# Residual stream and the outputs of w_out, w_down and the last projection with tokens on partitions, in a three-block fp32 kernel on one core

## The chip, the cores and the metric

One core of a Trainium2 chip runs the whole program in one launch. The metric is the device time in microseconds (us); a time is the median of several runs of the same kernel. The profile is of one execution. Engines are named as the profile does: PE (TensorE, matmul), PEld (its weight load), DVE (VectorE), ACT (ScalarE), POOL (GpSimd), SP (SyncE, which issues most DMAs).

## The reference, cut to what matters

256 tokens of width D = 2048 pass two layers of the first block and one of the second. All is float32.

```python
for l in range(2):                              # first block
    u = rms_norm(h, norm_pre_mix[l])
    p = u @ w_in[l]                             # four groups of mixers read p
    mixed = concat(o_ret, o_hgrn, o_ml, o_rw) @ w_out[l]             # 2048 x 2048
    h = h + rms_norm(mixed, norm_post_mix[l])
    u = rms_norm(h, norm_pre_ffn[l])
    ffn = (silu(u @ w_gate[l]) * (u @ w_up[l])) @ w_down[l]           # w_down: 5632 x 2048
    h = h + rms_norm(ffn, norm_post_ffn[l])
shift, scale, gate = split(c @ w_ada + b_ada)   # second block
u = rms_norm(h, g_pre) * (1 + scale) + shift
proj = u @ w_in_2                               # two attentions read it and give `merged`
return h + gate * rms_norm(merged @ w_out_2, g_post)
# rms_norm(x, g) = x * rsqrt(mean(x * x) + 1e-6) * g
```

## The kernel before, in words

**Weights.** Each weight is read once from HBM in chunks of 128 x 1024 (512 KB). `prep` sends a chunk by SP's queue to `raw` (a ring of 3), ScalarE rounds it to fp32r as `hi` (L104), VectorE subtracts for `lo` (L105); `hi` and `lo` are rings of 4. An activation is split the same way, so that a product is wh·xh + wh·xl + wl·xh.

**Two forms of a product.** In `stream_a` a block of 128 x 128 weights is stationary and the activations move, high and low part side by side: one matmul of 512 columns (L151) and one of 256 (L152) per block, output features on partitions, tokens in the free dimension. A job with `one` True makes three matmuls of 256 columns in their place (L147 to L149). In `stream_b` the activations are stationary and 512 columns of weights move, three matmuls for each half of the tokens (L195 to L197): tokens on partitions, two banks of 512 columns at the end. Before the change it serves the value and gate projections of the mixers.

**The residual stream.** `h` is [128 features, 16 blocks k, 256 tokens]. w_out, w_down and the last projection run as 16 jobs of 128 output features. `collect` takes each job's bank: ScalarE squares it (L219), GpSimd and VectorE add the squares up, VectorE writes the bank times the gain into `mo` (tiles named `uq`). At the end the matmul `mean` with a constant 1/D sums over partitions (L233); `rstd` makes the root as a tile R of 128 x 256 by Ln and Exp on ScalarE and one Newton step on VectorE (L252 to L263), while `busy` gives TensorE 20 matmuls on constants. Then `entry` feeds the next stage k by k: `residual` multiplies `mo` with R on GpSimd (on VectorE for k = 0, L313) and adds to `h` on VectorE (L314), `u_tile` makes the two parts of u, on ScalarE (L299) and VectorE (L300). The root of the *new* norm isn't waited for: u goes unscaled into the matmuls, and the results are scaled when their banks are drained; `late` squares `h` (L219) after the first stage's last group.

**The first stage of a consumer** (four jobs side by side, so that 4 k are 16 pairs of matmuls, a *group*) is the place where TensorE follows `feed`: `FIRST` has four groups of four k. Layer 0 has no residual: x comes by SP's queue in the layout of `h`, and `START` has five groups, the first with one k. The second block's entry uses tiles `u1` of its own with a column more for the shift.

**What sets the order.** The program is written stage by stage and ordered by a scheduler ahead of time; `issue_after` pins single instructions behind others.

Of the kernel before, what the change touches and what calls it, by code (L numbers as in the profile page):

```python
# [17 lines left out]
D = 2048  # L18
# [10 lines left out]
class Squares:  # L29


    def __init__(self):
        self.parts, self.bank, self.begun = [], None, False


class Core:
# [53 lines left out]
    def prep(self, srcs, n, pool=False):  # L90
# [14 lines left out]
        self.last = (nc.gpsimd if pool else nc.vector).tensor_tensor(lo[:, :n], raw[:, :n], hi[:, :n].bitcast(F32), op=OP.subtract)  # L105
        return hi, lo

    def stream_a(self, jobs, rhs, phases, feed=None, late=None, load=None, whole=None, bank=None):
# [10 lines left out]
        for ph in phases:  # L119
# [7 lines left out]
            with ExitStack() as cx:  # L127
# [3 lines left out]
                for i in range(0, len(jobs), step):  # L131
                    if soon and i and made:
                        cx.enter_context(self.tc.issue_after(self.squared.ins))
                    hi, lo = self.prep(w[i:i + step], n, soon and i > 0 and len(made) > 0)
                    parts += [(hi[:, j * n:(j + 1) * n], lo[:, j * n:(j + 1) * n]) for j in range(min(step, len(jobs) - i))]
# [47 lines left out]
    def stream_b(self, w, nk, lhs, done):  # L183

        nc = self.nc
        banks = [self.sbank() for _ in range(2)]
        for k0 in range(0, nk, 2):
            hi, lo = self.prep([w[:, k0 * 512:(k0 + 2) * 512]], 1024)
            for j in range(2):
                k = k0 + j  # L190
                x = lhs(k)
                for tt in range(2):
                    xh, xl = x[:, tt * 128:(tt + 1) * 128], x[:, 256 + tt * 128:384 + tt * 128]
                    wh, wl = hi[:, j * 512:(j + 1) * 512], lo[:, j * 512:(j + 1) * 512]
                    nc.tensor.matmul(banks[tt], xh, wh, start=(k == 0), stop=False)  # L195
                    nc.tensor.matmul(banks[tt], xh, wl, start=False, stop=False)  # L196
                    nc.tensor.matmul(banks[tt], xl, wh, start=False, stop=(k == nk - 1))  # L197
        for tt in range(2):
            done(tt, banks[tt])
# [15 lines left out]
    def square(self, acc, x, i, n):  # L215

        nc = self.nc
        sq = self.t(self.ev, [128, 256], f"acc{i}", 1) if i < 2 else self.t(self.ev, [128, 256], "sq", 2)
        self.squared = nc.scalar.square(sq, x)  # L219
        if i < 2 or i == n - 1:  # L220
            acc.parts.append(sq)
        else:
# [1874 lines left out]
```

## Time and profile before

| what | before |
|---|---|
| median of 3 runs | 3568.17 us (3563.52 to 3569.63) |
| profiled execution, time | 3567.99 us |
| profiled execution, span | 3565.9 us |
| mean granted TensorE clock | 0.989 of full speed |
| PE busy | 3481.8 us, 98% |
| DVE, ACT, POOL busy | 70%, 50%, 19% |
| weights read from HBM | 645.78 MB, 182 GB/s over the span |

The span runs from the first to the last instruction; the time has a little around it. A share of busy time is an average over stages: TensorE stands still at few places only, and each of them is short, so the table tells little of them and the timeline has to.

### The profile page before, as it was taken

How to read it: one execution, taken by the hardware profiler on the slowest of the kernel's cores; microseconds unless marked ns; L12 is line 12 of the kernel's file. 1: busy time of each engine (PE TensorE's matmuls, PEld its weight loads, DVE VectorE, ACT ScalarE, POOL GpSimd, SP SyncE). 2: the span in 40 equal slices, each digit the busy share in tenths (PEclk: the TensorE clock that was granted, in tenths of full speed). 3: DMA queues.
4: the chain of work that ended last, by engine and by line, in shares of the span. 5: the costliest groups of instructions: out<-in, count | busy, mean ns of one | idle time of the engine just before them, and what ended most of it. 6: DMA issues, size and time to landing. Idle time of an engine off the chain costs nothing.

```text
span 3565.9 us, 61722 instructions
## 1 busy us (share of the span) xinstructions
PE 3481.8 (98%) x23680; PEld 3055.1 (86%) x23680; DVE 2483.3 (70%) x4456; ACT 1769.4 (50%) x2957; POOL 660.2 (19%) x824
## 2 busy tenths in 40 slices
PE   8999999999999999999999899999999999999997
PEld 8788987888888888878888788888888899988886
DVE  7777877777776557887786877776556766765555
ACT  5553545544444444655455544444444654555443
POOL 2123303211110004122320411111003212100001
PEclk9999999999999999999999999999999999999999
DMA  6335555677776664424455577777664655445554
GB/s 207 114 107 165 181 169 152 222 235 235 237 236 211 206 195 153 157 81 148 158 169 183 168 234 234 238 235 227 205 201 150 197 166 167 140 136 186 187 184 141
DMA packets 209368, 652.46 MB, mean 183 GB/s; under 512 B 24176, under 2 KB 27152, under 8 KB 209072
## 3 DMA queue, kind: packets, MB, share of 16 engines
q1 hardware_dynamic: 169664, 577.84, 50.7%
q10 hardware_dynamic: 39408, 70.67, 6.2%
q8 instruction: 186, 3.05, 0.3%
q14 instruction: 110, 0.90, 0.1%
HBM read 645.78 MB, written 2.65 MB: 182 GB/s over the span
## 4 chain that ended last, share of the span: by engine, by line
PE 85%; DVE 8%; DMA 2%; ACT 2%; issue 2%; POOL 0%; ACTq 0%; SPq 0%; DVEq 0%; POOLq 0%
PE s L151 34%; PE s L152 17%; PE s L147 5%; PE s L149 5%; PE s L148 5%; PE s L195 4%; PE s L196 3%; PE s L197 3%; DVE lo L105 2%; DVE h L314 1%; ACT hi L104 1%; DMA raw<-in_wina_dram 1%; PE g L148 1%; PE g L149 1%; DVE uq L300 1%
## 5 line engine op out<-in xcount | busy, mean ns | idle before, releaser
L105 DVE TENSOR_TENSOR lo<-raw,hi 128x1024 fp32r<-128x1024 f32 (+1 forms) x1101 | 1383.9, 1258 | 834.4 <-ACT hi L104 827.4
L104 ACT CAST hi<-raw 128x1024 fp32r<-128x1024 f32 (+1 forms) x1105 | 1141.6, 1035 | 1275.5 <-PE s L151 676.1
L151 PE MATMUL s<-uq,hi 128*128 128x512 f32 x3344 | 1177.6, 394 | 3.9 <-ACT hid L211 3.9
L152 PE MATMUL s<-uq,lo 128*128 128x256 f32 x3344 | 934.6, 279 | 0.0
L151 PEld LDWEIGHTS s<-uq,hi 128*128 128x128 f32 x3344 | 628.3, 188 | 154.4 <-ACT hid L211 4.5
L152 PEld LDWEIGHTS s<-uq,lo 128*128 128x128 f32 x3344 | 628.4, 188 | 0.2
L151 PE MATMUL s<-hid,hi 128*128 128x512 f32 x1320 | 466.5, 396 | 0.0
L147 PE MATMUL s<-uq,hi 128*128 128x256 f32 x1456 | 418.6, 288 | 1.3 <-ACT hi L104 0.5
L148 PE MATMUL s<-uq,hi 128*128 128x256 f32 x1456 | 417.7, 287 | 0.0
L149 PE MATMUL s<-uq,lo 128*128 128x256 f32 x1456 | 417.4, 287 | 0.0
L152 PE MATMUL s<-hid,lo 128*128 128x256 f32 x1320 | 372.2, 282 | 0.0
L151 PEld LDWEIGHTS s<-hid,hi 128*128 128x128 f32 x1320 | 248.0, 188 | 60.1
L147 PEld LDWEIGHTS s<-uq,hi 128*128 128x128 f32 x1456 | 275.2, 189 | 9.3 <-issue 6.6
L149 PEld LDWEIGHTS s<-uq,lo 128*128 128x128 f32 x1456 | 275.3, 189 | 6.1 <-issue 5.1
L148 PEld LDWEIGHTS s<-uq,hi 128*128 128x128 f32 x1456 | 275.4, 189 | 5.9 <-issue 4.8
L152 PEld LDWEIGHTS s<-hid,lo 128*128 128x128 f32 x1320 | 247.9, 188 | 0.0
L196 PE MATMUL s<-lo,uq 128*128 128x512 f32 x608 | 245.4, 404 | 1.0 <-DVE lo L105 1.0
L195 PE MATMUL s<-hi,uq 128*128 128x512 f32 x608 | 242.8, 406 | 0.6 <-ACT vo L1867 0.4
L197 PE MATMUL s<-hi,uq 128*128 128x512 f32 x608 | 243.1, 401 | 0.0
L223 POOL TENSOR_TENSOR acc<-acc,sq 128x256 f32<-128x256 f32 x70 | 84.4, 1206 | 791.3 <-ACT sq L219 791.3
L373 POOL TENSOR_TENSOR gs<-e,R 128x256 f32<-128x256 f32 x88 | 81.0, 921 | 443.8 <-DVE e L206 408.3
L379 POOL TENSOR_TENSOR e<-e,R 128x256 f32<-128x256 f32 x88 | 76.1, 864 | 367.5 <-DVE e L206 367.5
(638 smaller groups left out, 5230.1 us busy)
## 6 DMA issues: line engine op xcount, KB each, us to landing
raw<-in_wg_dram SPq DMA_DIRECT2D x168, 512.0 KB, 4.5
raw<-in_wu_dram SPq DMA_DIRECT2D x168, 512.0 KB, 4.7
raw<-in_wd_dram SPq DMA_DIRECT2D x160, 512.0 KB, 3.6
raw<-in_wina_dram SPq DMA_DIRECT2D x154, 512.0 KB, 3.9
raw<-in_win2a_dram SPq DMA_DIRECT2D x130, 512.0 KB, 4.2
raw<-in_winb_dram SPq DMA_DIRECT2D x96, 512.0 KB, 3.6
raw<-in_wout_dram SPq DMA_DIRECT2D x96, 512.0 KB, 4.5
aw<-in_wada_dram ACTq DMA_DIRECT2D x192, 256.0 KB, 5.0
```

The source lines that it names most:

```text
L104: self.last_hi = nc.scalar.copy(hi[:, :n], raw[:, :n])
L105: self.last = (nc.gpsimd if pool else nc.vector).tensor_tensor(lo[:, :n], raw[:, :n], hi[:, :n].bitcast(F32), op=OP.subtract)
L147: nc.tensor.matmul(banks[i][:, 0:n], wh, x[:, 0:n], start=first, stop=False)
L148: nc.tensor.matmul(banks[i][:, 0:n], wh, x[:, n:2 * n], start=False, stop=False)
L149: nc.tensor.matmul(banks[i][:, 0:n], wl, x[:, 0:n], start=False, stop=last)
L151: nc.tensor.matmul(banks[i], wh, x, start=first, stop=False)
L152: nc.tensor.matmul(banks[i][:, 0:256], wl, x[:, 0:256], start=False, stop=last)
L195: nc.tensor.matmul(banks[tt], xh, wh, start=(k == 0), stop=False)
L196: nc.tensor.matmul(banks[tt], xh, wl, start=False, stop=False)
L197: nc.tensor.matmul(banks[tt], xl, wh, start=False, stop=(k == nk - 1))
L223: (nc.vector if i % 2 else nc.gpsimd).tensor_tensor(acc.parts[i % 2], acc.parts[i % 2], sq, op=OP.add)
L373: nc.gpsimd.tensor_tensor(g, e, rget(), op=OP.mult)
```

## The change

`h` becomes [128 tokens, 2 halves, 2048], and so does `mo`. w_out, w_down and the last projection become four blocks of 512 output features through `stream_b` (`rows_b`), with the weights laid out for it. ScalarE squares a bank and sums the squares along its row in the same instruction (`accum_out`); the root is a column [128,1] for each half of the tokens. The gain comes by a DMA as a tile of 128 x 512 for each block. The residual is one VectorE instruction (`h = mo * r + h`). For u the tokens must be back in the free dimension: `entry` transposes `h` on TensorE, 32 times 128 x 128 per entry, and u is read from the banks; `h` is squared in eight instructions of 128 x 512. The root of the entry is a column too and is spread to the tile R by one matmul (`Rstd`). In layer 0 x still comes transposed, into slots of `raw`, and `h` comes once more as one DMA of 2.1 MB on ScalarE's queue. `busy` drops from 20 to 10 matmuls. The second block keeps the scaled transposes as `hs`, and its output gain goes to DRAM once to be read back as a row.

```diff
+    def stream_b(self, w, ks, lhs, done, banks=None, apart=False, beside=None):
...
+            order = [(j, tt) for j in range(2) for tt in range(2)]
+            for j, tt in sorted(order, key=lambda x: x[1]) if apart and end else order:
...
+    def rows_b(self, ws, nk, lhs, gains, acc, sides, orders=None, beside=None):
+        nc = self.nc
+        self.new_mo()
+        for i in range(4):
+            gain = self.t(self.ev, [128, 512], "gain", 1)
+            with self.tc.issue_after(self.last_hi.ins):
+                nc.scalar.dma_start(gain, gains(i).partition_broadcast(128))
...
+            def done(tt, bank, i=i, gain=gain):
+                sq = self.t(self.ev, [128, 512], "sq", 1)
+                nc.scalar.activation(sq, bank, AF.Square, accum_out=acc.ss[:, tt, i:i + 1])
+                def keep():
+                    nc.vector.tensor_tensor(self.mo[tt][:, i * 512:(i + 1) * 512], bank, gain, op=OP.mult)
+                if i < 3:
+                    keep()
+                else:
+                    acc.later.append(keep)
...
+                if i == 3:
+                    x, t, y = acc.x[:, tt, 1:2], acc.x[:, tt, 2:3], acc.r[:, tt:tt + 1]
+                    nc.vector.scalar_tensor_tensor(x, acc.ss[:, tt, 3:4], 1.0 / D, acc.x[:, tt, 0:1], op0=OP.mult, op1=OP.add)
+                    nc.scalar.activation(y, x, AF.Ln)
+                    self.rooted = nc.scalar.activation(y, y, AF.Exp, scale=-0.5)
+                    self.newton(y, x, t)
+            side = sides[i]
+            self.stream_b(ws[i], orders[i] if orders else range(nk), lhs, done, None if side is None else [self.g(side), self.g(side)], i == 3, beside)
...
+    def warm(self):
+        with self.tc.issue_after(self.last_mm.ins):
+            self.busy(10)
...
+    def residual(self, acc, c):
+        for tt in range(2):
+            self.nc.vector.scalar_tensor_tensor(self.h[:, tt, c], self.mo[tt][:, c], acc.r[:, tt:tt + 1], self.h[:, tt, c], op0=OP.mult, op1=OP.add)
...
         def feed(ph):
-            for k in ph:
-                if r is not None:
-                    self.residual(k, r, k == 0)
-                made = self.u_tile(u(k) if u else self.uk(k), self.h[:, k], w[:, k:k + 1], r is not None and k == 0)
-            return made if r is not None else ()
+            if x is None and ph[0] == 8:
+                for f in mo.later:
+                    f()
+            for i, k in enumerate(ph):
+                if x is None:
+                    if i == 0 or k == 1:
+                        self.residual(mo, slice(k * 128, 128 if k == 0 else (ph[-1] + 1) * 128))
+                    if i % 2 == 0:
+                        g = self.g()
+                    turned[k] = v = g[:, i % 2 * 256:i % 2 * 256 + 256]
+                    for tt in range(2):
+                        nc.tensor.transpose(v[:, tt * 128:(tt + 1) * 128], self.h[:, tt, k * 128:(k + 1) * 128], self.ident)
...
         def late():
-            for k in range(KT):
-                self.square(acc, self.h[:, k], k, KT)
+            for tt in range(2):
+                for i in range(4):
+                    sq = self.t(self.ev, [128, 512], "sq", 1)
+                    nc.scalar.activation(sq, self.h[:, tt, i * 512:(i + 1) * 512], AF.Square, accum_out=acc.ss[:, tt, i:i + 1])
             rs()
...
+        if ph[0] == 8:
+            with tc.issue_after(K.last_hi.ins):
+                nc.scalar.dma_start(K.h, A["xn"])
```

How the scheduler has ordered the work around the first seam (w_out of layer 0 into its feed-forward) is seen in the instruction lists. VectorE before, from the end of the root (R) on; `uq<-h` are halves of u:

```order
L263 SCALAR_TENSOR_TENSOR R<-tmp,R 128x256
L313 TENSOR_TENSOR tmp<-uq,R 128x256
L314 TENSOR_TENSOR h<-h,tmp 128x256 x2
L297 TENSOR_SCALAR uq<-h,nrm 128x256
L300 SCALAR_TENSOR_TENSOR uq<-h,nrm,uq 128x256
L314 TENSOR_TENSOR h<-h,tmp 128x256
L300 SCALAR_TENSOR_TENSOR uq<-h,nrm,uq 128x256
```

VectorE after, at the same place (`sr` is the new root, `uq<-g` a low half of u read from transposes, `nx` and `Rn` the entry's root):

```order
L281 SCALAR_TENSOR_TENSOR sr<-sx,sr 128x1 x2
L317 SCALAR_TENSOR_TENSOR h<-uq,sr,h 128x128
L317 SCALAR_TENSOR_TENSOR h<-uq,sr,h 128x384
L317 SCALAR_TENSOR_TENSOR h<-uq,sr,h 128x128
L317 SCALAR_TENSOR_TENSOR h<-uq,sr,h 128x384
L317 SCALAR_TENSOR_TENSOR h<-uq,sr,h 128x512 x6
L312 SCALAR_TENSOR_TENSOR uq<-g,nrm,uq 128x256 x3
L446 TENSOR_REDUCE nx<-ss 128x2
L447 TENSOR_SCALAR nx<-nx 128x2
L279 SCALAR_TENSOR_TENSOR nx<-Rn,nx 128x2
L280 TENSOR_TENSOR nx<-nx,Rn 128x2
L281 SCALAR_TENSOR_TENSOR Rn<-nx,Rn 128x2
```

Before, residuals and halves of u take turns; after, all ten pieces of the residual stand ahead of the first low half of u, and the entry's root stands ahead of the fourth. ScalarE at the same place, before (after `R` the squares of `h`, L219, and the high halves of u, L299, take turns):

```order
L252 ACTIVATE R<-g,cc 128x256
L254 ACTIVATE R<-R 128x256
L219 ACTIVATE acc_7503<-h 128x256
L299 ACTIVATE uq<-h,nrm 128x256
L219 ACTIVATE acc_7505<-h 128x256
L299 ACTIVATE uq<-h,nrm 128x256
```

ScalarE after (L363 are the squares of `h`, L311 the high halves of u, L108 the weights' `hi`):

```order
L108 CAST hi<-raw 128x1024
L363 ACTIVATE sq,ss<-h 128x512
L311 ACTIVATE uq<-g,nrm 128x256 x2
L363 ACTIVATE sq,ss<-h 128x512 x5
L311 ACTIVATE uq<-g,nrm 128x256
L363 ACTIVATE sq,ss<-h 128x512 x2
L448 ACTIVATE Rn<-nx 128x2
L449 ACTIVATE Rn<-Rn 128x2
L311 ACTIVATE uq<-g,nrm 128x256 x5
```

The eight squares of 128 x 512 and the Ln and Exp of the entry's root now all stand ahead of the fourth high half of u. The third place is ScalarE at the start of the program, before (L1240 loads a table of vectors):

```order
L104 CAST hi<-raw 128x768 x2
L1240 DMA vec<-in_vec_dram 128x86
L299 ACTIVATE uq<-h,nrm 128x256 x4
L219 ACTIVATE sq<-h 128x256 x2
L299 ACTIVATE uq<-h,nrm 128x256 x4
```

and after, where u is made from slots of `raw`, and L1375 is the load of `h`:

```order
L108 CAST hi<-raw 128x1024 x2
L1375 DMA h<-in_xn_dram 128x4096
L311 ACTIVATE uq<-raw,nrm 128x256 x4
L363 ACTIVATE sq,ss<-h 128x512 x3
L108 CAST hi<-raw 128x1024
L363 ACTIVATE sq,ss<-h 128x512
```

Three squares, which need that load, stand ahead of the next cast of weights.

## Rows read from the trace of the kernel before

**Rows 1.** The profile's page: the span, and busy time of each engine.

```profile
span 3565.9 us, 61722 instructions
...
PE 3481.8 (98%) x23680; PEld 3055.1 (86%) x23680; DVE 2483.3 (70%) x4456; ACT 1769.4 (50%) x2957; POOL 660.2 (19%) x824
```

**Rows 2.** Windows, four seams: length, PE, PEld, DVE, ACT, POOL busy, clock, DMA, GB/s.

```profile
594.50:665.00 70.50, 60.10 (x302) 50.68 (x302) 59.05 (x89) 37.05 (x69) 32.09 (x31) 0.93 0.46 151
1359.50:1405.00 45.50, 37.59 (x256) 35.13 (x257) 41.57 (x59) 24.07 (x46) 28.90 (x36) 0.92 0.38 128
1969.10:2035.00 65.90, 56.38 (x282) 47.72 (x282) 57.18 (x86) 35.81 (x67) 32.09 (x31) 0.92 0.47 152
2732.80:2785.00 52.20, 44.90 (x315) 42.57 (x315) 47.18 (x76) 29.64 (x57) 24.65 (x24) 0.93 0.37 120
```

**Rows 3.** Timeline of PE, first seam: start, length, instruction, [idle before <- releaser].

```profile
594.24 0.28 PE L149 MATMUL s<-mix,lo 128*128 128x256 f32 x1
...
602.94 0.50 PE L151 MATMUL g<-uq,hi 128*128 128x512 f32 x1 [2.19 <-DVE uq L300]
...
618.62 0.62 PE L151 MATMUL g<-uq,hi 128*128 128x512 f32 x1 [3.91 <-DVE uq L300]
```

**Rows 4.** Window behind that stop, same columns as in rows 2.

```profile
618.70:622.20 3.50, 3.50 (x11) 2.96 (x12) 3.50 (x6) 3.01 (x6) 2.77 (x4) 0.52 0.47 170
```

**Rows 5.** Groups of DVE, 594 to 640 us: busy us, mean ns | idle before.

```profile
L314 DVE TENSOR_TENSOR h<-h,tmp 128x256 f32<-128x256 f32 x16 | 11.2, 711 | 0.0
```

**Rows 6.** Window inside the feed-forward, L151 alone: length, PE, PEld, clock, DMA, GB/s.

```profile
1120.00:1340.00 220.00, 220.00 (x624) 116.98 (x623) 1.00 0.64 199
```

**Rows 7.** Timeline of PE at three other places.

```profile
398.06 0.60 PE L564 MATMUL g<-ident,o 128*128 128x128 f32 x4
...
2799.67 0.39 PE L196 MATMUL s<-lo,uq 128*128 128x512 f32 x1
...
2805.76 0.40 PE L195 MATMUL s<-hi,uq 128*128 128x512 f32 x1
...
3540.81 0.28 PE L147 MATMUL s<-mg,hi 128*128 128x256 f32 x1
...
3546.09 0.28 PE L149 MATMUL s<-mg,lo 128*128 128x256 f32 x1
```

**Rows 8.** Groups of DVE, 480 to 560 us.

```profile
L105 DVE TENSOR_TENSOR lo<-raw,hi 128x1024 fp32r<-128x1024 f32 x28 | 34.2, 1224 | 19.6 <-ACT hi L104 19.6
...
L664 DVE TENSOR_TENSOR o<-o,hms 128x512 f32<-128x512 f32 x4 | 2.6, 688 | 0.1
...
L262 DVE TENSOR_TENSOR hmt<-hmt,hms 128x16 f32<-128x16 f32 x6 | 1.0, 175 | 0.2
```

**Rows 9.** Groups of ACT over the whole span.

```profile
L1698 ACT ACTIVATION_READ_ACCUMULATOR p<-p,sst 128x1 f32 x64 | 12.0, 187 | 0.0
...
L1017 ACT COPY wdc<-wD 64x4 f32<-64x4 f32 x32 | 6.2, 192 | 0.3
...
L1915 ACT ACTIVATE zth<-s 128x512 f32<-128x512 f32 x8 | 4.7, 596 | 2.8 <-PE s L197 2.5
```

**Rows 10.** Timeline of the end, all engines.

```profile
3546.87 0.28 PE L149 MATMUL s<-mg,lo 128*128 128x256 f32 x1
...
3547.25 0.38 ACT L219 ACTIVATE sq<-s 128x256 f32<-128x256 f32 x1 [4.84 <-PE s L149]
...
3560.53 0.68 DVE L2056 TENSOR_TENSOR uq<-uq,R 128x512 f32<-128x512 f32 x1
...
3561.13 1.28 DVE L2057 TENSOR_TENSOR h<-h,uq 128x512 f32<-128x512 f32 x2
```

**Rows 11.** Waits of PE, 0 to 40 us: us, times, longest.

```profile
PE g L147 <- ACT hi L104: 9.5, 4, 4.7
```

**Rows 12.** Window at the start, columns as in rows 2.

```profile
5.00:16.00 11.00, 8.48 (x46) 7.99 (x46) 8.25 (x16) 8.56 (x21) 2.21 (x3) 0.84 0.97 349
```

**Rows 13.** Timeline of ACT at the start.

```profile
24.51 1.03 ACT L104 CAST hi<-raw 128x1024 fp32r<-128x1024 f32 x1
```

More of the change, by code (lines that the diff above doesn't have):

```diff
@@ L26, with __init__ @@
 EPS = 1e-6
-class Squares:
-    def __init__(self):
-        self.parts, self.bank, self.begun = [], None, False
+class Sums:
+    def __init__(self, K):
+        self.ss = K.t(K.ev, [128, 2, 4], "ss", 2)
+        self.x = K.t(K.ev, [128, 2, 3], "sx", 2)
+        self.r = K.t(K.ev, [128, 2], "sr", 2)
+        self.later = []
 class Core:
@@ L104, in prep @@
         self.last_hi = nc.scalar.copy(hi[:, :n], raw[:, :n])
-        self.last = (nc.gpsimd if pool else nc.vector).tensor_tensor(lo[:, :n], raw[:, :n], hi[:, :n].bitcast(F32), op=OP.subtract)
+        with ExitStack() as cx:
+            for x in after:
+                cx.enter_context(self.tc.issue_after(x.ins))
+            self.last = nc.vector.tensor_tensor(lo[:, :n], raw[:, :n], hi[:, :n].bitcast(F32), op=OP.subtract)
         return hi, lo
@@ L212, in split @@
         self.nc.vector.tensor_tensor(dst[:, 256:512], src, dst[:, 0:256].bitcast(F32), op=OP.subtract)
[L215 to L222, printed above, removed]
-            (nc.vector if i % 2 else nc.gpsimd).tensor_tensor(acc.parts[i % 2], acc.parts[i % 2], sq, op=OP.add)
-    def means(self, acc, last):
-        if acc.bank is None:
-            acc.bank = self.g()
-        if len(acc.parts) > 1:
-            self.nc.vector.tensor_tensor(acc.parts[0], acc.parts[0], acc.parts[1], op=OP.add)
-            acc.parts.pop(1)
-        for i, a in enumerate(acc.parts):
-            acc.mm = self.nc.tensor.matmul(acc.bank[:, 0:256], self.mean, a, start=(i == 0 and not acc.begun), stop=(last and i == len(acc.parts) - 1))
-        acc.parts, acc.begun = [], True
     def busy(self, n):
@@ L389, in ffn @@
             beside()
[L390 to L399 removed]
+    acc = Sums(K)
+    K.rows_b(wd, FT, hid, gains, acc, (0, None, 0, None), beside=beside)
     return acc
@@ L410, in __call__ @@
         if self.r is None:
-            self.r = self.K.rstd(self.acc)
+            K, nc = self.K, self.K.nc
+            n = self.nat()
+            d = K.t(K.ev, [128, 256], "tmp", 2)
+            for tt in range(2):
+                nc.vector.tensor_scalar(d[:, tt * 128:(tt + 1) * 128], K.ident, n[:, tt:tt + 1], float(D), op0=OP.mult, op1=OP.mult)
+            g = K.g()
+            nc.tensor.matmul(g[:, 0:256], K.mean, d, start=True, stop=True)
+            self.r = K.t(K.ev, [128, 256], "R", 1)
+            nc.scalar.copy(self.r, g[:, 0:256])
         return self.r
@@ L1246, in columns, with mixers @@
     return V
-def mixers(K, l, A, entry, wcols, dram, V):
+def mixers(K, l, A, entry, dram, V):
     nc, tc = K.nc, K.tc
@@ L1785, in block2 @@
             nc.gpsimd.tensor_copy(u1[:, :, i], zero)
-        feed, late, rs, _ = K.entry(scl, r, lambda k: u1[:, k])
+        feed, late, rs, _ = K.entry(scl, mo, lambda k: u1[:, k], keep=hs)
         def first(i):
@@ L1833, in run_b @@
     def run_b(done):
-        K.stream_b(wb[next(jb)], KT, K.uk, done)
+        K.stream_b(wb[next(jb)], range(KT), K.uk, done)
     cc = ExitStack()
```

237 lines of the change are left out of this document (107 added, 130 removed).

## The prediction

> **What bounds the kernel now.** I began with the busy shares. TensorE is busy for 3481.8 of 3565.9 us [rows 1]: only removing matmul time, or one of the few places where TensorE stands, can move the end. The waits of TensorE over the whole span lie at the start, at the four places where one block's output becomes the next block's input (I call them seams: w_out to feed-forward and w_down to the next entry, twice each), and after the last matmul. For each seam I took one window that begins just after the last accumulating matmul and ends when the next stage runs smoothly, and counted TensorE's instructions in it [rows 2]. In the first, 302 matmuls less the 20 of `busy` and 8 with `mean` leave 137 pairs of a 512- and a 256-column matmul. A pair costs 0.353 us (220 us for 624, [rows 6]), so 48.3 of 70.5 us are work and 22.2 us are lost. The third loses 21.1 us in the same way. The second and fourth run 256-column matmuls, 0.120 us each (44 steps in 5.28 us, [rows 7]): 230 and 289 of them, 17.9 and 17.5 us lost. The seams together lose 79 us.
>
> Inside the first seam the timeline shows what the loss is made of [rows 3]: 8.70 us from the last matmul (594.24) to the first of the next stage (602.94), released by VectorE's low half of `u`; later a stop of 3.91 us, again for that half. After it TensorE's granted clock is 0.52, its lower level of 1.2 GHz instead of 2.4, for 3.5 us [rows 4]. VectorE is why: one residual add of 128x256 takes 711 ns there [rows 5], though 512 columns of a two-tensor operation take 688 elsewhere [rows 8]; GpSimd computes the other factor of the same residual meanwhile.
>
> **The change, part by part.** *Matmuls.* Four 128-column jobs become one 512-column block: per k, 4 pairs (1.411 us) become 6 matmuls of 512 columns. These stand 0.2342 us apart (26 steps in 6.09 us, [rows 7]), 1.405 us. On 44 k by 4 blocks that saves 1.1 us per w_down, with 0.3 more because the last job ran in 256-column form (0.360 for 0.353); w_out has five such jobs, so 0.4 + 0.6; the last projection 0.5. In all 2.8 + 2.0 + 0.5 = 5 us. Weight bytes and the hi/lo split per byte are the same, and VectorE and ScalarE have room in these stages.
>
> *A seam after.* Time 0 is the issue of the last matmul. A 256-column bank was read 0.38 us after its last matmul's issue (3546.87 to the square at 3547.25); for 512 columns I take 0.5. The square takes 0.60 like another 512-column read of a bank, and its accumulator must be read out, 0.19 [rows 9]: 1.3. One small VectorE operation (0.17, [rows 8]), Ln and Exp on 128x1 (0.19 each by the smallest ScalarE copy, [rows 9]) and three Newton steps of 0.17: 2.5. Then comes what the order shows and the code does not: VectorE does *all* residuals, eight operations with 2 x 2048 columns, before the first low half of `u`. 512 columns start 0.60 us apart [rows 10], so 8 x 0.60 and two extra starts of 0.1 are 5.0: 7.5. One half of `u` (0.69 for 512 columns [rows 8] less 0.3 for the half of them, and 0.1 as it reads a bank: 0.5) and TensorE starts at about 8.1. Before it was 8.7: the chain through the small root gains 5 us and the block of residuals spends them.
>
> TensorE then waits once more. ScalarE has the eight squares of `h` (0.6 + 0.19 = 0.8 each, rather than sixteen short ones spread over the whole stage) mixed into the first group: two `u`, five squares, one `u`, two squares, Ln, Exp, and only then `u` of k = 3. It starts at 3.4 and can read the first transposes at 4.5: 2 x 0.45 (a 256-column bank was read in 0.38 [rows 10], starts a little further apart), 5 x 0.8, 0.45, 2 x 0.8 bring it to 11.5; VectorE's sum 0.35, Ln and Exp 0.4, `u` 0.45: 12.7. VectorE adds its half (0.5) and the low part of the second weight chunk (1.22, [rows 8]): 14.4. Eight of the group's 16 pairs are left, 2.8 us, and half a microsecond of transposes: the group ends at 17.7 instead of the 5.6 of its matmuls alone, so 12.1 us are lost. In the other groups VectorE needs 1.7 us for four `u` and 2.4 for two low parts, under TensorE's 5.6; TensorE pays for the 24 transposes left, 0.11 us each (four in 0.60 with 0.27 for the last one's length, [rows 7]), 2.6 us, and 0.2 for the matmul that spreads the root. The pause before k = 3 is like that in [rows 3], so 1.6 us for the low clock. A seam then loses 16.5 us. Where u's two parts pass through a third copy (entry of the second block), ScalarE alone has 8 x 0.8 + 16 x 0.45 + 16 x 0.41 + 6 casts of 1.0 [rows 13] = 26 us of work from 3.4 on, so it ends near 30, and TensorE 3 to 4 later: 33.5 less 23 is 10.5, plus waits and clock 15. The four: 16.5 + 16.7 (ScalarE also issues two DMAs there) + 16.5 + 15 = 65, a gain of 14 us. Bounds: if the squares do not delay `u`, 12 each, a gain of 31; if every wait comes as long as before, a loss of 1.
>
> A rule of the Trainium skill (TensorE: Matmul & The Clock Gate, Part 4, PE-mode transpose) speaks against the change: transposes do not count as TensorE being busy in the way matmuls do, and the full clock does not engage for them. In this trace eight transposes sit between full-speed matmuls (from 398.06) and the matmuls after them stay 0.12 us apart. By the rule the result would be the third rival below.
>
> *The end.* Now 3565.9 - 3546.87 = 19.0 us follow the last matmul's issue [rows 1, 10]. After: square of the second token half read out at 1.3, small step 1.5, the gain product 2.2, four residuals of the first half (its root is ready, as its matmuls are done 1.4 us earlier) to 4.6, Newton 5.1, four residuals 7.5. From the end of the last VectorE operation now (3561.13 + 1.28) to the end of the span are 3.5 us for the last output transfer: 11.0, so 8 us gained. If the eight output transfers are held up by one another, 5.5; if the first half's four are done before the second's bank is ready, 8.5.
>
> *The start.* Before, four stops for the weights' high part take 9.5 us [rows 11], at 349 GB/s [rows 12]. `x` now takes slots of the three `raw` buffers, and `h` comes as one more 2.1 MB, on ScalarE's queue. In ScalarE's order three squares of that `h` stand ahead of the weights' fourth group. 2.1 MB with 1.5 MB of other chunks in flight need 10 us at 349 GB/s. Issued near 14 (the third group's casts done early, as the ring holds back less data) they land at 24 to 26, the squares take 2.4, and the cast that was at 24.51 [rows 13] comes at 27 to 28: 4 us lost. Bounds: 0 (other stops hide it) and 8 (`h` issued only at 18).
>
> *At nothing*: the gain's DMA, the product with the gain and the squares of the first three blocks (a block's own 22 to 62 us of matmuls cover them; without cover 0.8 to 1.3 us a block, at most 20 in all), and the reordering that the scheduler makes inside the mixers, of either sign.
>
> Sum: 5 + 14 + 8 - 4 = 23. The profiled execution took 3567.99 (span 3565.9 and 2.1 around it), like the median 3568.17: **3545 us**.
>
> **Rivals.** (1) *The seams stay as long as they are*: what the residual block and the squares cost is all that the shorter root gives. For it: my own 8.1 against 8.7. Against: GpSimd leaves VectorE alone, and the later groups have room. Then 5 - 1 + 8 - 4 = 8: 3560. (2) *The squares hide*: 12 us per seam, 3528. For it: nothing waits for the root until the first job is drained. Against: ScalarE's order. (3) *Slower, low clock through the entries*: `busy` is halved to 10 and eight transposes break each group. If the 48 pairs after the first group ran at the low level, each would cost 0.29 us more (0.64, as 11 pairs' matmuls fill 3.5 us in [rows 4]), 13.9 a seam, 56 in all: 3601. It decides from about 20 of 64 pairs per seam (23 us / 4 / 0.29). Against it: the low stretch in [rows 4] ends by itself after 3.5 us, under stops like those I expect. The skill's rule stands behind this one. (4) *The start alone*: `h` lands late and holds ScalarE 8 us longer than I take: 3553.
>
> **How the numbers follow.** Forecast 55%, (1) 15%, (2) 15%, (3) 7%, (4) 8%. A measurement tells some 0.2%, 7 us, from no change, so faster is under 3561: the forecast, (2) and (4), and over half of (1), 0.85; the same 0.07, slower 0.08. The sum of the good bounds is 31 + 8.5 + 5 = 44.5 (3523) and of the bad -1 + 5.5 + 5 - 8 = 1.5 (3566). The range from 3526 to 3562 leaves out the low clock, the worst of (1) and the very best of (2).
>
> **What would show it.** In the changed profile: 512-column matmuls 0.234 us apart through w_down; at each seam about 8 us from the last matmul to the first, ended by VectorE's `u`, with six residual operations just ahead of it; a second wait of some 2 us inside the first group with ScalarE in squares; 11 us after the last matmul; and ScalarE waiting for `h` between 16 and 26 us. I am wrong if the first matmul of a seam comes before 6 us, if the granted clock stays near 0.5 past the first group, if the start stretches by over 8 us, or if the stages between, which do the same work in another order, differ by over 5 us.

## The result

The changed kernel takes 3530.51 us, median of 4 runs (3526.97 to 3532.25), beside 3568.9 of the kernel before (3563.52 to 3569.99): a ratio of 0.9894, interval 0.9877 to 0.9911. I had forecast 3545 and a gain of 23; the gain is 38, in the spans 36.1. The page of the changed kernel, span and busy times [against rows 1]:

```profile
span 3529.7 us, 58684 instructions
...
PE 3464.4 (98%) x22379; PEld 2984.8 (85%) x22379; DVE 2379.7 (67%) x4287; ACT 1749.2 (50%) x2900; POOL 493.6 (14%) x686
```

TensorE's busy time fell by only 17 us of the 36, so half of the gain is time in which it had stood. Where it went is read from the first and last matmul of each stage (worked out from the starts of the matmuls in both traces; us):

| stretch | before | after | difference | forecast |
|---|---|---|---|---|
| start to the 192nd matmul on u | 38.24 | 44.51 | +6.3 | +4 |
| from there to w_out of layer 0 | 463.25 | 462.21 | -1.0 | 0 |
| w_out, twice | 185.5 | 182.97 | -2.5 | -2.0 |
| w_down, twice | 498.1 | 492.32 | -5.8 | -2.8 |
| last projection | 92.03 | 89.66 | -2.4 | -0.5 |
| seam and feed-forward, layer 0 | 515.91 | 511.10 | -4.8 | seams -14 |
| seam and mixers, layer 1 | 516.92 | 511.34 | -5.6 | |
| seam and feed-forward, layer 1 | 514.63 | 508.39 | -6.2 | |
| seam and second block | 722.29 | 716.46 | -5.8 | |
| last matmul to the end | 18.99 | 10.78 | -8.2 | -8 |

The first seam on TensorE's timeline [against rows 3]; L270 are the matmuls on constants, L348 transposes:

```profile
598.20 0.40 PE L208 MATMUL s<-hi,mix 128*128 128x512 f32 x1
598.43 2.46 PE L270 MATMUL g<-mean 128*128 128x512 f32 x10
...
606.76 0.69 PE L348 MATMUL g<-ident,h 128*128 128x128 f32 x2 [4.04 <-DVE uq L312]
607.10 0.78 PE L159 MATMUL g<-uq,hi 128*128 128x512 f32 x1
```

8.90 us from the last matmul to the first, where it was 8.70, ended by VectorE's low half of u. VectorE's timeline there:

```profile
600.66 5.65 DVE L317 SCALAR_TENSOR_TENSOR h<-uq,sr,h 128x128 f32<-128x128 f32 x10
606.23 0.87 DVE L312 SCALAR_TENSOR_TENSOR uq<-g,nrm,uq 128x256 fp32r<-128x256 f32 x2
```

The root is done 2.5 us after the last matmul, and the ten residual pieces then take 5.65. ScalarE's timeline, with the squares of `h` (L363) and the high halves of u (L311) of k = 2 and 3:

```profile
607.88 0.45 ACT L311 ACTIVATE uq<-g,nrm 128x256 fp32r<-128x256 f32 x1
...
608.98 0.63 ACT L363 ACTIVATE sq<-h 128x512 f32<-128x512 f32 x1
...
610.48 0.47 ACT L311 ACTIVATE uq<-g,nrm 128x256 fp32r<-128x256 f32 x1
```

The last square begins 10.8 us after the last matmul and u of k = 3 is ready after 12.75, as worked out (12.7). But TensorE does not stop for it: its granted clock is 0.50 over the first six pairs, so it arrives later. Windows of the first group and of the four stretches of [rows 2], shifted to the new times (the first of the four is 2.5 us shorter):

```profile
607.10:611.40 4.30, 4.30 (x16) 3.72 (x15) 1.54 (x7) 3.32 (x12) 0.00 (x0) 0.50 0.00 0
611.50:615.00 3.50, 3.50 (x23) 3.07 (x22) 2.03 (x6) 0.47 (x1) 0.00 (x0) 0.98 0.27 92
...
598.43:666.43 68.00, 61.49 (x339) 52.75 (x338) 46.22 (x85) 38.11 (x75) 7.00 (x8) 0.95 0.50 162
1355.69:1401.19 45.50, 41.32 (x301) 38.67 (x299) 30.21 (x58) 24.38 (x52) 8.45 (x19) 0.92 0.37 126
1958.52:2024.42 65.90, 60.44 (x339) 51.98 (x338) 47.02 (x85) 38.26 (x75) 7.00 (x8) 0.97 0.50 165
2713.07:2765.27 52.20, 49.89 (x375) 46.82 (x374) 40.94 (x84) 39.33 (x89) 7.25 (x8) 0.97 0.42 134
```

Less 32 transposes, 10 constants and 2 records of the matmul that spreads the root, these hold 147.5 pairs, 257 matmuls of 256 columns, 147.5 pairs and 331: 15.9, 14.7, 13.8 and 12.5 us lost, 57 in all, where it was 79 and I had forecast 65. The first window ends where a second low stretch begins, behind a stop for the bank that VectorE drains with L257:

```profile
665.24 0.50 PE L159 MATMUL s<-uq,hi 128*128 128x512 f32 x1 [1.77 <-DVE e L257]
666.00:669.00 3.00, 3.00 (x12) 2.56 (x11) 2.05 (x3) 1.62 (x3) 0.00 (x0) 0.54 0.62 224
```

At the old length of 70.5 us the first seam loses 17.0, the four 58.

### The profile page after: what moved, and what is told of

The parts are those of the page before. It is cut to its first block, busy times and chain, and to the rows that moved or that the text cites. A ratio compares the mean times of both kernels' runs of the same rounds, so it can differ in the third digit from the quotient of the medians.

```text
span 3529.7 us, 58684 instructions
## 1 busy us (share of the span) xinstructions
PE 3464.4 (98%) x22379; PEld 2984.8 (85%) x22379; DVE 2379.7 (67%) x4287; ACT 1749.2 (50%) x2900; POOL 493.6 (14%) x686
## 4 chain that ended last, share of the span: by engine, by line
PE 89%; DVE 5%; DMA 2%; ACT 2%; issue 1%; POOL 0%; ACTq 0%; DVEq 0%; SPq 0%; POOLq 0%
PE s L159 22%; PE s L160 11%; PE s L206 7%; PE s L207 7%; PE s L208 7%; PE s L157 4%; PE s L155 4%; PE s L156 4%; PE g L206 4%; PE g L208 4%; PE g L207 4%; DVE lo L112 1%; PE g L159 1%; ACT hi L108 1%; DMA raw<-in_wina_dram 1%
## 5 line engine op out<-in xcount | busy, mean ns | idle before, releaser
L108 ACT CAST hi<-raw 128x1024 fp32r<-128x1024 f32 (+1 forms) x1089 | 1139.5, 1049 | 1294.6 <-PE s L159 333.6
L159 PE MATMUL s<-uq,hi 128*128 128x512 f32 x3168 | 1112.9, 394 | 3.0 <-DVE e L257 3.0
L160 PE MATMUL s<-uq,lo 128*128 128x256 f32 x3168 | 885.9, 280 | 0.0
L159 PEld LDWEIGHTS s<-uq,hi 128*128 128x128 f32 x3168 | 594.9, 188 | 145.1 <-DVE e L257 4.0
L160 PEld LDWEIGHTS s<-uq,lo 128*128 128x128 f32 x3168 | 594.6, 188 | 0.3 <-DVE lo L112 0.2
L157 PE MATMUL s<-uq,lo 128*128 128x256 f32 x1440 | 414.8, 288 | 0.0
L157 PEld LDWEIGHTS s<-uq,lo 128*128 128x128 f32 x1440 | 273.1, 190 | 10.0 <-issue 8.3
L156 PEld LDWEIGHTS s<-uq,hi 128*128 128x128 f32 x1440 | 273.6, 190 | 5.8 <-issue 4.7
L155 PEld LDWEIGHTS s<-uq,hi 128*128 128x128 f32 x1440 | 272.8, 189 | 4.8 <-issue 2.6
L207 PE MATMUL s<-lo,uq 128*128 128x512 f32 x672 | 270.6, 403 | 2.7 <-DVE lo L112 2.7
L206 PE MATMUL s<-hi,uq 128*128 128x512 f32 x672 | 268.2, 405 | 3.5 <-ACT vo L1901 3.0
L208 PE MATMUL s<-hi,uq 128*128 128x512 f32 x672 | 268.5, 401 | 0.0
L206 PEld LDWEIGHTS s<-hi,uq 128*128 128x128 f32 x672 | 127.8, 191 | 36.3 <-ACT vo L1901 3.4
L207 PEld LDWEIGHTS s<-lo,uq 128*128 128x128 f32 x672 | 128.2, 191 | 32.6 <-DVE lo L112 3.1
L208 PEld LDWEIGHTS s<-hi,uq 128*128 128x128 f32 x672 | 127.9, 190 | 30.1 <-issue 1.2
L206 PE MATMUL s<-hi,hid 128*128 128x512 f32 x352 | 139.3, 396 | 0.0
L208 PE MATMUL s<-hi,hid 128*128 128x512 f32 x352 | 139.3, 396 | 0.0
L208 PE MATMUL g<-hi,hid 128*128 128x512 f32 x352 | 139.3, 396 | 0.0
```

Of the source, the lines that this page charges most:

```text
L108: self.last_hi = nc.scalar.copy(hi[:, :n], raw[:, :n])
L155: nc.tensor.matmul(banks[i][:, 0:n], wh, x[:, 0:n], start=first, stop=False)
L156: nc.tensor.matmul(banks[i][:, 0:n], wh, x[:, n:2 * n], start=False, stop=False)
L157: nc.tensor.matmul(banks[i][:, 0:n], wl, x[:, 0:n], start=False, stop=last)
L159: nc.tensor.matmul(banks[i], wh, x, start=first, stop=False)
L160: nc.tensor.matmul(banks[i][:, 0:256], wl, x[:, 0:256], start=False, stop=last)
```

## The experiments

Each is the changed kernel with one edit (shown shortened), if nothing else is said; ratios are against the kernel before on the same chip. An edit reaches further than its own lines: in all but after_again, busy0 and h_late the scheduler also orders ScalarE's and VectorE's work in the mixers of layer 1, between 1500 and 1900 us, in another way than in the kernel that it edits. Spans and medians hold that too. In the table below, `first` is the time from the last matmul of a stage to the first on u, `400th` that to the 400th matmul on u, a point behind the first stage and its drains.

| kernel | median us | ratio, interval | 192nd at the start | first, four seams | 400th, four seams |
|---|---|---|---|---|---|
| before | 3568.9 | 1 | 38.24 | 8.70, 8.61, 8.70, 7.87 | 92.99, 73.03, 91.72, 67.59 |
| changed | 3530.51 | 0.9894, 0.9877-0.9911 | 44.51 | 8.90, 6.81, 8.89, 5.47 | 88.18, 69.22, 85.48, 62.59 |
| after_again | 3529.62 | 0.9884, 0.987-0.9899 | 45.17 | 8.90, 6.82, 8.90, 5.47 | 85.30, 69.62, 86.56, 61.23 |
| split | 3523.62 | 0.9869, 0.9854-0.9884 | 45.78 | 5.27, 4.94, 5.26, 5.47 | 83.75, 67.00, 83.97, 62.49 |
| sq_seam | 3568.51 | 0.9989, 0.998-0.9997 | 44.55 | 8.90, 6.80, 8.90, 5.46 | 95.17, 77.78, 94.36, 66.78 |
| before_dve | 3557.58 | 0.9962, 0.9948-0.9975 | 38.38 | 8.22, 7.96, 8.21, 7.20 | 88.34, 71.43, 88.74, 62.77 |
| busy22 | 3523.99 | 0.9868, 0.9854-0.9881 | 44.61 | 8.76, 6.82, 8.75, 7.05 | 84.09, 68.40, 86.35, 60.82 |
| busy0 | 3526.69 | 0.9872, 0.9858-0.9886 | 45.65 | 8.90, 6.96, 8.91, 5.47 | 85.76, 68.86, 85.12, 62.93 |
| apart0 | 3526.25 | 0.988, 0.9863-0.9896 | 43.93 | 8.90, 4.78, 8.90, 5.47 | 86.49, 68.88, 86.97, 62.92 |
| sq_start | 3527.56 | 0.9878, 0.9864-0.9891 | 44.80 | 8.91, 6.81, 8.90, 5.47 | 87.09, 68.23, 85.83, 63.00 |
| h_late | 3530.66 | 0.9885, 0.9872-0.9898 | 45.59 | 8.91, 6.95, 8.90, 5.47 | 87.39, 68.28, 85.36, 62.68 |
| h_last | 3527.03 | 0.9872, 0.9859-0.9885 | 39.00 | 8.90, 6.95, 8.90, 5.47 | 85.81, 68.50, 85.79, 62.71 |
| split_turned | 3512.56 | 0.9841, 0.9827-0.9856 | 38.18 | 5.26, 4.94, 5.26, 5.46 | 84.40, 65.41, 82.60, 62.31 |
| split_turned_sq | 3518.42 | 0.9857, 0.9843-0.9872 | 38.08 | 5.27, 4.94, 5.27, 5.47 | 83.96, 65.46, 87.49, 60.84 |

**Once more, unaltered** (after_again).

> The changed kernel once more, unaltered, for a second profile. Theory A (the stages with the mixers and attentions vary from one execution to the next by some 3 us each, since with the same instructions in the same order layer 0's took 459.0 to 466.0 us in four profiles): seams, w_out, w_down, the last projection and the end repeat within 0.3 us, the long stages differ by 1 to 4 us. Theory B (executions repeat, and the differences seen came from the edits): every stage within 0.5 us.

Theory A. The first matmul of a seam, w_out, w_down, the last projection and the end repeat within 0.02 us; the long stages differ by 0.4 to 2.9 (feed-forward of layer 0 behind its first matmul 502.20 and 499.32). But behind the 400th matmul on u both feed-forwards take 422.92 us in both profiles, as in the kernel before, and the mixers of layer 1 442.12 and 442.15: what varies there lies in the first 400, where the clock falls. The stretches of the first seam whose clock was 0.50 and 0.54 in the changed kernel's profile, in the second one:

```profile
607.23:611.53 4.30, 4.30 (x21) 3.74 (x20) 1.54 (x7) 3.30 (x12) 0.00 (x0) 0.70 0.00 0
666.13:669.13 3.00, 3.00 (x19) 2.64 (x18) 2.05 (x4) 2.55 (x4) 0.00 (x0) 1.00 0.82 238
```

So differences under some 3 us in one entry of the column 400th say nothing, and the -1.0 behind the 192nd matmul in the first table is none.

**The block of residuals** (split).

```diff
-                        self.residual(mo, slice(k * 128, ...))
+                        with ExitStack() as order:
+                            if ph[0]:
+                                order.enter_context(self.tc.issue_after(low[min(ph[0], 8) - 1].ins))
+                            self.residual(mo, slice(k * 128, ...))
```

> The residual of k = 4 to 7 is pinned behind VectorE's low half of u for k = 3, that of k = 8 to 15 behind that of k = 7; nothing else is changed. Theory A (the block of ten residual pieces is what a seam now waits for): at the first seam four pieces (some 2.1 of the 5.65 us) stand ahead of u instead of ten, so the first matmul comes 5.3 us after the last of w_out instead of 8.9; the third seam the same, the second and fourth gain 1 to 3 each; in all 9 to 11 us, a span near 3520. Theory B (the work is only moved: later groups then stop for their own residuals): new stops before k = 4 or k = 8 eat it, under 1 us per seam, a span of 3526 to 3530.

Theory A for the first matmul, theory B in part for what follows. The timeline of VectorE with the pin:

```profile
599.63 1.67 DVE L317 SCALAR_TENSOR_TENSOR h<-uq,sr,h 128x128 f32<-128x128 f32 x4
...
606.39 1.41 DVE L317 SCALAR_TENSOR_TENSOR h<-uq,sr,h 128x512 f32<-128x512 f32 x2
```

Four pieces in 1.67 us stand ahead of u, and TensorE starts 5.27 us after the last matmul, 3.63 earlier than in the changed kernel (1.87, 3.63 and 0 in the others, where the fourth starts on high halves alone). By the 32nd matmul the first seam is 6.0 us ahead (11.07 for 17.02), by the 96th only 2.4 (27.7 for 30.1): TensorE now stops ahead of k = 4 and of k = 8, for VectorE's low half of u, which comes behind the residuals moved there:

```profile
609.93 0.44 PE L352 MATMUL g<-ident,h 128*128 128x128 f32 x2 [0.97 <-DVE uq L312]
...
618.42 0.44 PE L352 MATMUL g<-ident,h 128*128 128x128 f32 x2 [1.76 <-DVE uq L312]
```

By the 400th matmul the first three are ahead of the changed kernel by 4.4, 2.2 and 1.5, and of its second profile by 1.6, 2.6 and 2.6: some 7 us of the 9 to 11 arrive. The ratios give 5 to 9 us (0.9869 for 0.9884 and 0.9894), with intervals that overlap.

**The squares** (sq_seam).

```diff
+                    with ExitStack() as order:
+                        if x is None:
+                            order.enter_context(self.tc.issue_after(high[-1].ins))
-                    nc.scalar.activation(sq, self.h[...], AF.Square, ...)
+                        nc.scalar.activation(sq, self.h[...], AF.Square, ...)
```

> At the four seams the eight squares of h are pinned behind ScalarE's last high half of u; the start of the program is as in the changed kernel. Theory A (the squares hide: they run while VectorE is in the residuals, and TensorE at its lower clock needs k = 3 later than it is ready): span within 2 us of 3529.7, perhaps 1 to 2 longer, as the entry's root R comes 6 us later and the first drains wait for it. Theory B (my prediction's step: the squares ahead of u for k = 3 hold the first group up): 2 us less per seam, a span near 3522.

Both are wrong in the sum: nearly the whole gain is lost. The first group isn't touched (the 32nd matmul 17.13 us after the last one, 17.02 in the changed kernel), so the squares did not hold it up, as theory A said. The price stands later, in TensorE's waits of 602 to 675 us:

```profile
PE g L441 <- DVE tmp L439: 7.7, 1, 7.7
```

L441 is the matmul that spreads the entry's root. It has its fixed place in TensorE's queue, the root now comes late, and the matmuls behind it wait too (whether they would have had free banks in that time no run shows): 7.7 us here, 7.4 at the third seam, 2.6 in the second. The column 400th shows 7.0, 8.6, 8.9 and 4.2 us more, 29 of the 37 us by which the span is longer. The early squares that I booked as a cost are what keeps this matmul from stopping TensorE.

**GpSimd beside VectorE** (before_dve; the kernel *before*).

```diff
-        (nc.vector if fast else nc.gpsimd).tensor_tensor(t, self.mok(k), r, op=OP.mult)
+        nc.vector.tensor_tensor(t, self.mok(k), r, op=OP.mult)
```

> The kernel before with the residual's product on VectorE for every k; GpSimd then has only squares to add there. Theory A (the add of 128 x 256 takes 711 ns on VectorE because GpSimd computes beside it, while 512 columns take 688 elsewhere): the adds of L314 fall to 430 to 480 ns and product plus add take 0.9 us for each k, a little more than 0.71 alone, so the seams stay within 3 us each of before, span 3560 to 3575. Theory B (the add is slow by itself, as it reads and writes h in place): adds stay at 0.7, product and add are 1.1 or more, each seam is 6 us longer, span near 3590.

Theory A, and more than it: groups of VectorE in the first seam [against rows 5]:

```profile
L313 DVE TENSOR_TENSOR tmp<-uq,R 128x256 f32<-128x256 f32 x16 | 7.4, 484 | 0.0
L314 DVE TENSOR_TENSOR h<-h,tmp 128x256 f32<-128x256 f32 x16 | 6.4, 416 | 0.0
```

The add falls from 711 to 416 ns. The Trainium skill (SBUF — State Buffer, SBUF: two separate sides) has a rule for it: a VectorE operation with two inputs in SBUF and a GpSimd one that reads SBUF lock each other out for a whole instruction. The two numbers agree with it in that the add is slower beside GpSimd; that it is a lock for whole instructions they don't show. A hint, no more, as the profile's spans on GpSimd are rough, that it goes both ways: GpSimd's own add of squares rises from 986 ns in the kernel before to 1700 in before_dve (594 to 632 us in both):

```profile
L223 POOL TENSOR_TENSOR acc<-acc,sq 128x256 f32<-128x256 f32 x8 | 7.9, 986 | 12.0 <-ACT sq L219 12.0
...
L223 POOL TENSOR_TENSOR acc<-acc,sq 128x256 f32<-128x256 f32 x7 | 11.9, 1700 | 18.1 <-ACT sq L219 18.1
```

VectorE does more and TensorE is served sooner: by the 400th matmul the seams gain 4.7, 1.6, 3.0 and 4.8, 14 us in all, where the whole change gains 4.8, 3.8, 6.2 and 5.0, 20 us (23 in its second profile). The profiled execution is among the fastest of its six (3552.78, median 3557.58); the median too is 14 us under that of the kernel before on the same chip. So over half of what the change won in the seams is to be had without the new layout, by that one line.

**The clock** (busy22, busy0): 22 matmuls on constants in place of 10, and none.

```diff
     def warm(self):
         with self.tc.issue_after(self.last_mm.ins):
-            self.busy(10)
+            self.busy(22)
```

> 22 matmuls on constants after the last block instead of 10. In the changed kernel the first eight pairs of the first and third seam stand 0.64 us apart instead of 0.353, 2.3 us per seam. Theory A (TensorE's clock fell because it had almost nothing to do between 600.9 and 607.1): 22 end near 603.6, the transposes still come before VectorE is done with the residuals, and the first pairs run at the full clock: 2 us per seam, a span of 3522 to 3526. Theory B (the three microseconds left before u are enough for the clock to fall): no change within 1 us. Theory C (the transposes are late by 2.7 us and hold u up): 1 to 2 us longer per seam.

> No matmuls on constants at the seams. Theory A (TensorE's low clock after a pause ends by itself under the first matmuls and transposes): the first group of each seam loses up to 2 us more, the later groups nothing; span 3530 to 3538. Theory B (my third rival: with transposes between them the matmuls don't bring the full clock back): the whole entry runs at 1.2 GHz, about 14 us per seam more, span near 3580.

Windows of busy22 at the first seam, then at the third:

```profile
600.60:603.80 3.20, 0.48 (x4) 0.25 (x3) 3.20 (x6) 2.69 (x9) 0.00 (x0) 1.00 0.01 3
603.80:607.00 3.20, 3.12 (x19) 2.57 (x19) 1.01 (x5) 3.08 (x10) 0.00 (x0) 1.00 0.00 0
...
1953.60:1956.90 3.30, 0.59 (x6) 0.35 (x5) 3.30 (x7) 2.79 (x9) 0.00 (x0) 1.00 0.00 0
1956.90:1960.10 3.20, 3.20 (x14) 2.82 (x14) 0.98 (x4) 3.06 (x10) 0.00 (x0) 0.61 0.00 0
```

After the same 3.2 us of near rest the clock holds in one seam (16th matmul 12.10 us after the last one; 13.96 in the changed kernel) and falls to 0.61 in the other (13.30; 13.23). Theory A holds once, theory B once; the span is 9.0 shorter, but up to the end of the seams' first stages only 4.3 of it have come; the rest lies in long stages, which vary. Windows of busy0 at the first seam:

```profile
605.40:609.70 4.30, 4.30 (x16) 3.72 (x15) 1.56 (x7) 3.31 (x12) 0.00 (x0) 0.50 0.00 0
609.80:613.00 3.20, 3.20 (x20) 2.85 (x20) 1.70 (x6) 0.47 (x1) 0.00 (x0) 0.97 0.23 79
```

Without constants the low level lasts the same 4.3 us as in the changed kernel and is over in the next window, with transposes in between. The ten matmuls buy nothing, and my third rival (theory B of busy0) is out.

**The last two k** (apart0): the halves are drained together.

```diff
-            for j, tt in sorted(order, key=lambda x: x[1]) if apart and end else order:
+            for j, tt in order:
```

> The last two k of a block in the ordinary order and the two halves drained after both, so that the first half of the tokens is done 0.7 us before the second instead of 1.4. Theory A (the root's chain counts: two squares of 0.8 us stand one behind the other): the end is 0.5 to 0.8 us longer than 10.78, and the first u of the first and third seam 0.5 to 0.8 later than 8.90. Theory B (the residuals that follow on VectorE hide it): the end within 0.2 us.

Theory B: the end takes 10.96 for 10.78, the first seam 8.90 as before. What ends last in both places is VectorE's block of residuals, not the root. (The second seam's first matmul comes 2.0 us earlier, its 16th at 12.05 for 12.09.)

**The start** (sq_start, h_late, h_last).

```diff
 # sq_start: squares of h in layer 0
+                        if x is not None:
+                            order.enter_context(self.tc.issue_after(self.last_hi.ins))
 # h_late: the same, and
-        if ph[0] == 8:
+        if ph[0] == 12:
 # h_last: the load of h too moves behind the last cast, to the place of the squares
```

> In layer 0 alone the eight squares of h are pinned behind the last cast of weights of the first stage; the load of h stays where it is. Theory A (the start loses its time because ScalarE stands 5.4 us for h with casts of weights queued behind the squares): TensorE's stop of 7.5 us at 22.8 shrinks to 1 or 2, and the 192nd matmul comes near 39 us instead of 44.5; a span near 3524. Theory B (the 2.1 MB of h take the DMA engines from the weights, wherever the squares stand): the stop only changes its name to the weights' DMA, gain under 2 us.

> In layer 0 the 2.1 MB load of h is issued behind the casts of the third chunk pair (k = 8 to 11) instead of the second, and the squares of h stand behind the last cast of the first stage. Theory A (at the start the DMA engines are the limit: with the squares late but the load where it was, the chunk of x for k = 8 to 11 kept ScalarE waiting 9.1 us and nothing was won): now only the last chunk of x meets the load; the 192nd matmul at 40 to 42 us instead of 44.5. Theory B (all of the load has to pass in the same first 45 us, wherever it is issued): 192nd matmul at 44 to 46.

> In layer 0 the load of h is issued behind the last cast of the first stage, the squares behind it. Theory A (DMA engines are the limit of the first stage): the stage runs as in the kernel before, the 192nd matmul at 38 to 39 us. The price is a later root: ScalarE has casts of the next stage behind squares that wait for h, so a new stop of up to 5 us may come near 45 us; at the 336th matmul (65.4 in the changed kernel, 59.5 before) 61 to 66. Theory B (something else than h holds the first stage up): 192nd matmul at 43 or later.

In the changed kernel ScalarE's timeline shows what I had drawn from the order, with a cast of weights behind squares that wait (in rows 13 it was at 24.51):

```profile
16.54 0.33 ACTq L1375 DMA_DIRECT2D h<-in_xn_dram  x1
...
27.27 0.63 ACT L363 ACTIVATE sq<-h 128x512 f32<-128x512 f32 x1 [5.35 <-DMA h<-in_xn_dram]
...
29.41 1.03 ACT L108 CAST hi<-raw 128x1024 fp32r<-128x1024 f32 x1
```

Yet taking the squares away changes only the name of the wait. ScalarE's timeline of sq_start:

```profile
16.51 0.35 ACTq L1380 DMA_DIRECT2D h<-in_xn_dram  x1
26.68 1.70 ACT L311 ACTIVATE uq<-raw,nrm 128x256 fp32r<-128x256 f32 x4 [9.13 <-DMA raw<-in_x_dram]
```

Theory B: the 192nd matmul stays at 44.8. With the load one group later it stays at 45.6 (h_late, theory B). With the load behind the stage (h_last) it comes at 39.0, as theory A had it, but then ScalarE stands for h with casts queued behind; the waits of 0 to 60 us:

```profile
ACT sq L366 <- DMA h<-in_xn_dram: 7.5, 1, 7.5
...
PE s L155 <- ACT hi L108: 5.4, 1, 5.4
```

and the 336th matmul is at 65.6, as in the changed kernel (65.4; 59.5 before). So the first stage loses its 6 us to the bytes: 2.1 MB at the 349 GB/s of [rows 12] are 6.0 us. Behind that stage the order counts too: in h_last by the stop just shown, and with the load early and the squares late the 336th matmul comes at 63.0 (sq_start) and 63.3 (h_late), where the seven profiles with the changed kernel's start have 64.1 to 68.6. By w_out nothing of this is left: 508.4 and 507.9 us, beside 503.6 to 510.6.

**No second copy** (split_turned, split_turned_sq): the pin of split, and layer 0's `h` is loaded in pieces and transposed on TensorE as in the other entries; the second also has the pin of sq_start.

```diff
-            raw = self.t(self.wp, [128, 1024], "raw", 3)
-            nc.sync.dma_start(raw[...], x[:, ph[0]:ph[-1] + 1])
+            c = slice(ph[0] * 128, (ph[-1] + 1) * 128)
+            nc.sync.dma_start(self.h[:, :, c], x[:, :, c])
...
-                nc.scalar.dma_start(K.h, A["xn"])
```

> Residuals pinned as in the first experiment, and in layer 0 no second copy: h comes alone, 512 KB with each group, and u is made from transposes as in the other entries. Theory A (the start lost 6 us because 2.1 MB more have to pass at 349 GB/s): the 192nd matmul comes at 38 to 42 us instead of 44.5 (32 transposes cost 3.5 us, partly in waits), span 3515 to 3519. Theory B (the start loses to the squares and the layout of the load, 512 bytes per row): 44 or later, span 3521 or more.

> As the one before, with layer 0's squares of h pinned behind the last cast of the first stage. Theory A (squares that stand ahead of casts cost TensorE 1 to 3 us at the start): the 192nd matmul 1 to 3 us earlier than without the pin, span 3513 to 3518. Theory B (the root comes later and the matmul that spreads it holds TensorE's queue, as at the seams): what is won by the 192nd matmul is lost by the 336th.

Theory A of the first: the 192nd matmul at 38.18, 6.3 us earlier, transposes included, with one long wait of TensorE left in the first 60 us:

```profile
PE g L350 <- DMA h<-in_xn_dram: 3.5, 1, 3.5
```

At 3512.56 us, 0.9841 of before, it is faster than both kernels: 17 us under the changed kernel on the same chip (after_again). Six of the 19 us between the two profiles lie in the mixers of layer 1 behind the 400th matmul (436.1 for 442.1); split, with the same order there, has 440.3, so at least four of these six come with the execution and not with the edit. Pinning the squares there as well changes nothing at the start (38.08, 336th 55.76 for 55.64), so neither of its theories holds; its median is 6 us longer. Of the 9 us between the two profiles 5 lie in layer 0 between the first stage and w_out, where one has a stretch at the low clock and the other, at the same place, has none (split_turned_sq, then split_turned):

```profile
198.40:212.10 13.70, 13.70 (x172) 11.00 (x158) 9.19 (x31) 5.12 (x16) 2.28 (x3) 0.50 0.15 41
...
198.40:212.10 13.70, 13.39 (x199) 10.77 (x199) 10.96 (x38) 6.48 (x21) 3.39 (x5) 1.00 0.28 78
```

Whether the pin brings that about, one profile of each cannot tell.

## Why the prediction was right in its direction and short by 15 us

**The end: right.** 8.2 for 8. TensorE's last matmul, VectorE's two blocks of residuals (L2081) and the eight output DMAs in the changed kernel's timeline [against rows 10]:

```profile
3518.96 0.39 PE L208 MATMUL s<-hi,mg 128*128 128x512 f32 x1
...
3520.78 2.73 DVE L2081 SCALAR_TENSOR_TENSOR h<-uq,sr,h 128x512 f32<-128x512 f32 x4
3521.55 5.55 SPq L2099 DMA_DIRECT2D out_dram<-h  x8
...
3524.00 2.74 DVE L2081 SCALAR_TENSOR_TENSOR h<-uq,sr,h 128x512 f32<-128x512 f32 x4
```

The second block ends at 7.8 after the last matmul (forecast 7.5): its pieces take 0.68 each, not 0.60.

**A seam's first wait: right in the first and third seam.** The root at 2.5, the block of residuals, u at 8.1: measured 2.5, 5.65 for 5.0, and 8.9. split shows that the block is the cause. In the second and fourth the first matmul comes at 6.81 and 5.47, the fourth under the 6 us that I had named as a sign of being wrong: there TensorE starts with four matmuls on high halves alone, which I had not seen, and its fifth comes 1.8 and 2.8 us later.

**The first group: right in its end, wrong in what fills it.** I had it end at 17.7 us, with a stop before k = 3, and added 1.6 for a low clock *behind* that stop. Its 32nd matmul starts at 17.02. The low clock comes first, under the six pairs that follow the wait, and while it lasts k = 3 is made ready; the group has no stop and no second low stretch. The 1.6 was thus counted besides a delay that already contained it, some 5 us in the four seams, most of the difference between 58 and 65. By the 400th matmul TensorE is 20 us ahead (23 in the second profile) where I had 14: 6 to 9 of the 15 us by which the forecast was short. That the first seam's sum is nearly right, 17.0 for 16.5, is luck: the stop and the low stretch at its drains, which I had at nothing, fill the place. The squares' times were right to a tenth, but they were not what TensorE waited for (sq_seam).

**Matmul time: the mechanism right, the size too small.** I took 0.2342 us for 512 columns from a stretch of 26 steps. w_down's last matmul starts 1055 steps after its first:

```profile
1109.30 0.39 PE L206 MATMUL g<-hi,hid 128*128 128x512 f32 x1
...
1355.46 0.40 PE L208 MATMUL s<-hi,hid 128*128 128x512 f32 x1
```

246.16 / 1055 is 0.2333. Over 2 x 1056 matmuls that is 1.9 us; and the `mean` matmuls, which stood inside the last job of w_down and of the last projection, went too (0.4 us in each of the three by the gaps of the trace), with a stop of 1.4 us inside the last projection of the profile before. The term is 10.7 for 5 (its own parts add up to 5.3); about 1 us of the difference stays open.

**The start: the place right, the cause half wrong.** I had the copy land late and hold the casts up through ScalarE's order (4 us). At the 192nd matmul it costs 6, and there the bytes count and the place of the squares doesn't; the order has its share only behind that (sq_start, h_late, h_last).

**The rivals.** The seams did not stay as they were (79 to 58). That the squares hide was right for the first group (sq_seam), and its 3528 is the nearest to the time, but by luck: it had 48 us lost, and the rest comes from the matmul term. The low clock did not spread, though a pair cost the 0.64 us that I took for it (the Trainium skill, TensorE: Matmul & The Clock Gate, Part 4, PE-mode transpose, stood behind that one: in busy0 the clock is back at 0.97 in a stretch that holds two transposes between pairs; what transposes alone would do no run shows). The start cost 2 us more than I took, not 8. One thing no rival had: the matmul that spreads the root stops TensorE when the root is late. In the changed kernel it isn't.

That GpSimd slows VectorE in the seams, which I had read from 711 against 688 ns, is shown by before_dve. That taking it away is alone worth over half as much as the seams gained is shown for the kernel before; how much each part of the change adds on top of it was not run one by one, so this split of the seams' gain is argued. Not settled: why the clock held in one seam of busy22 and fell in another after the same rest, and why low stretches come at other places from one execution to the next, which is much of what varies between profiles.

## What to carry to other kernels

Before a layout is changed to shorten a seam, look whether two engines disturb each other in it: a slow VectorE operation beside a busy GpSimd was worth 14 us by one line. When a chain is cut, look in the instruction order for what the scheduler puts in the freed place: here the whole residual stood ahead of the first quarter that was needed. Then look behind that place: work that is pinned to a later one can stop the engine there, and about half of what split had won by the 32nd matmul was gone by the 400th. An instruction on the queue of the bounding engine is due whenever its place comes, and what stands behind it waits with it. A copy that is loaded while the DMA engines are the limit costs the stage its bytes, wherever it is issued in it. And before an edit is judged by the total, compare the order of instructions and the clock in the stages that it was not meant to touch.

## What the runs showed of the hardware that I had not expected

An add of 128x256 on VectorE took 711 ns while GpSimd multiplied in the same stretch and 416 when it did not; the other operation there (L300, two inputs of 256 columns) 689 and 597. After a rest of 3.2 us with four to six transposes in it, the granted clock of the matmuls behind it was 1.00 once and 0.61 once, in the same program. The same instructions in the same order took 499.3 and 502.2 us in a stage of 500 in two executions, while each seam's first matmul repeated to 0.01 and the last 422.92 us of the stage exactly; in the first 90 us the clock was 0.50 and 0.54 in two stretches of the longer one, 0.70 and 1.00 in the other.
